# Two rests of the first gate/up chunk on GpSimd, and two rests of later chunks behind the last seven-product pair

## The chip, the cores and the metric

The kernel runs on one core of a Trainium2 chip. The metric is the device time of one execution, in microseconds (us); lower is better. A core has several engines with a queue of instructions each: TensorE (PE) multiplies, VectorE (DVE), ScalarE (ACT) and GpSimd (POOL) work on elements, and SyncE (SP) issues most DMA transfers. Operands lie in SBUF, sums of matmuls in the banks of PSUM.

## The reference

Two layers over 256 tokens of width 2048, in float32. Each layer mixes the tokens (two kinds of attention, one output projection), and then runs a SwiGLU feed-forward part of width 5632. The case is in the second of these lines and what leads up to it:

```python
x = x + rms_norm(mixed, post_mix_norm[l])
h = rms_norm(x, pre_ffn_norm[l])
f = (jax.nn.silu(h @ w_gate[l]) * (h @ w_up[l])) @ w_down[l]
x = x + rms_norm(f, post_ffn_norm[l])
```

## The kernel before

**Numbers in two parts.** TensorE multiplies rounded numbers (the type fp32r). To reach float32 accuracy, every operand is split: `hi` is the value rounded by ACT (L307), `lo` is the rest, raw minus hi, taken as a rule by DVE (L317). I call the first the rounding and the second the rest of a weight. A product a times b becomes three matmuls: hi by hi, hi by lo, lo by hi (`product`, L1131 to L1136, and `eight`, L1252). The activations x have hi and lo as well: `columns` turns a block of x on TensorE (`turned_x`, the PE transposes of L502), ACT rounds the columns with the norm's gain (`rounded_x`, L508), and DVE takes their rests (`rest_of_x`, L516), which read one operand in PSUM and one in SBUF.

**Weights.** All weights stand in DRAM in the order of their use, in pieces of 128 x 1024 (two 128-row blocks by 512 columns, 512 KB), numbered through the whole program. `fetch` loads them by SP's queue into four `raw` buffers (L241), `feed` rounds them and takes their rests into six `hi` and six `lo` buffers. Gate/up has 11 chunks of 512 columns, and in each 8 pairs kp of row blocks, each with a gate weight and an up weight. In layer 0, chunk 0 starts at weight 128, chunk 1 at 144, chunk 2 at 160; the gate weight of a pair has the even number.

**Seven products in place of eight.** Some pairs are computed with a scheme of Strassen's kind: seven block products rather than eight, for sums that DVE must form first. `mixed_weights` (L263) does it for the weights: with gate G and up U, the tile T is U with the first half of G added to its own first half. SP loads U (L257), and an accumulating DMA on GpSimd's queue adds the half of G on top (L258, `accum_op`; it is the row `POOL L258 DMA_DIRECT2D`). Then DVE makes further sums (L290, L291), ACT rounds them (`Th`, L279) and DVE takes their rests (`Tl`, L281): `Tl` of the half T2 first (128 x 512), then of the pair in G (128 x 1024). For x, `pair_sums` adds hi and lo (`f`, L1377, two operands in SBUF) and `token_sums` makes four sums with their rounding (`sh`, L1151) and rests (`sl`, L1152). `seven_products` issues the 21 matmuls; the product p7 (t3) is the first to read the second `Tl`. After the last seven-product pair of a chunk, `shared_part` (L1175 to L1179) puts the four shared sums together for the evacuation of the chunk's banks (L1430 to L1436).

Chunk 0 takes its pairs in the order 0, 1, 3, 2, 7, 4, 6, 5, of which only 6 is a seven-product pair (weights 140 and 141). Chunk 1 takes 0 to 7, with 4, 5, 6 as seven-product pairs; its last is kp 6 (weights 156 and 157), and kp 7 (158 and 159) follows it as an ordinary pair. Chunk 2 has 2, 4, 5, 6 (its last: 172 and 173); chunks 3 to 9 have 2 to 6.

**The order of the work.** A scheduler orders each engine's queue. The code bends it where it names an instruction to issue behind: `tc.issue_after(...)`. The list `held` (an instruction and a count) tells `feed` that the next so many ordinary rests on DVE go behind that instruction; so far it is set once per chunk at the end of `shared_part`. The dictionary `newest_rest` holds each seven-product weight's newest rest, which after `mixed_weights` is the second `Tl`.

**GpSimd.** From chunk 1 on, two rests per chunk run on GpSimd (L310, the list `helped`): the gate weights of the second and third pair of the chunk (in layer 0: 146 and 148, then 162 and 164). The first of them gets a dependency on the newest seven-product matmul, `tc.add_manual_dep(..., reason="the shared port")`. Otherwise GpSimd issues the accumulating DMAs.

**The start of the feed-forward part.** Before chunk 0 a stretch is written out by hand (up to L1325): x is rescaled piece by piece (`rescaled`, L654), turned and rounded, while PE already works on the first pairs. `rounded_next` (L322) rounds the next weight and returns a function that takes its rest on an engine of choice, DVE if none is named. Behind it come the pair kp 3, then the other half of x's columns, the groups cg 3 and 2 for both token blocks t (16 column roundings, 16 column rests), and then the pair kp 2 and the loop over the chunks.

Of the kernel before, what the change touches and what calls it, by code (L numbers as in the profile page):

```python
# [13 lines left out]
ALU = mybir.AluOpType  # L14
# [7 lines left out]
NT = S // P  # L22
# [30 lines left out]
AFTER = mybir.DependencyInfo(mybir.DependencyClass.Sync, mybir.DependencyReason.DATA)  # L53
# [20 lines left out]
def gate_order(c):  # L74

    if c in MORE_AT:
        return MORE_ORDER
    return FIRST_ORDER if c == 0 else tuple(range(KT // 2))


def weight_order():

    order = []

    def queue_pair(name, l, kp, c):
        order.append((name, l, kp, c))
        return len(order) - 1

    plan = []
    sevens, plain, own = set(), set(), set()  # L90
    for l in range(L):
        lay = {"in": {}, "o": {}, "gate": {}, "up": {}, "down": {}}
        for n, (ca, cb) in enumerate(PAIRS):
            for kp in IN_ORDER if n else range(KT // 2):
                lay["in"][ca, kp] = queue_pair("w_in", l, kp, ca)
                lay["in"][cb, kp] = queue_pair("w_in", l, kp, cb)
                if kp in IN_NOW[n]:
                    plain.add(lay["in"][cb, kp])
        order_o = [(c, kp) for kp in KP_O for c in (0, 1)]
        order_o += [(c, kp) for kp in LATE_O for c in (2, 3)] + [(c, kp) for c in (2, 3) for kp in LAST_O]  # L100
        lay["order_o"] = order_o
        for c, kp in order_o:
            lay["o"][c, kp] = queue_pair("w_o", l, kp, c)
            if c == 3 and kp in O_SEVEN:
                own.add(lay["o"][c, kp])
        for c in range(FF // CW):
            for kp in gate_order(c):
                lay["gate"][c, kp] = queue_pair("w_gate", l, kp, c)
                lay["up"][c, kp] = queue_pair("w_up", l, kp, c)
                if kp in gate_sevens(c):  # L110
                    sevens.add(lay["up"][c, kp])
        for half in range(2):
            for kp in range(FF // P // 2):
                for c in (2 * half, 2 * half + 1):
                    lay["down"][c, kp] = queue_pair("w_down", l, kp, c)
                if kp in DOWN_SEVEN[half]:
                    sevens.add(lay["down"][2 * half + 1, kp])
        plan.append(lay)
    return order, plan, sevens, plain, own
# [48 lines left out]
def kernel(  # L168
# [15 lines left out]
    nc = tc.nc  # L184
# [19 lines left out]
    order, plan, sevens, plain, own = weight_order()  # L204
# [3 lines left out]
    for lay in plan:  # L208
        for c in range(1, FF // CW):
            for n in (1, 2):  # L210
                helped[lay["gate"][c, gate_order(c)[n]]] = n == 1
    newest_seven = [None]

    ready = {}
    raws, loads = [], []
# [2 lines left out]
    def fetch(upto):  # L218
        while len(raws) < min(upto, len(stream)):
            i = len(raws)  # L220
            for j in range(i, min(i + EARLY + 1, mix_raw[3])):
                if j in sevens and j not in sums:
                    summed(j)
            if i in sevens:
                raws.append(sums[i])
                continue
            if i + 1 in sevens:
                g = mix_raw[0].tile([P, 2, CW], F32, tag="G", bufs=mix_raw[1], name=f"G{i}")
                with not_ahead(i):
                    loads.append(nc.sync.dma_start(g, stream[i]))  # L230
                raws.append(g)
                continue
            if i in own or i + 1 in own:
                raw = mix_pool[0].tile([P, 2, CW], F32, tag="v", bufs=2, name=f"V{i}")
            elif i in plain or i + 1 in plain:
                raw = late_room([P, 2, CW], f"GU{i}")
            else:
                raw = wpool.tile([P, 2, CW], F32, tag="raw", bufs=4, name=f"raw{i}")
            mixing = bool({i, i + 1} & (own | plain))
            with not_ahead(i) if mixing else nullcontext():  # L240
                loads.append(nc.sync.dma_start(raw, stream[i]))  # L241
            raws.append(raw)
            if not mixing:
                usual.append((i, loads[-1]))
# [18 lines left out]
    def mixed_weights(i):  # L263

        g, u = raws[i - 1], raws[i]
        hi = wpool.tile([P, 2, CW], F32R, tag="hi", bufs=6, name=f"hi{i}")
        lo = wpool.tile([P, 2, CW], F32R, tag="lo", bufs=6, name=f"lo{i}")
        if i in own:
            th = wpool.tile([P, 2, CW], F32R, tag="hi", bufs=6, name=f"Th{i}")
            tl = wpool.tile([P, 2, CW], F32R, tag="lo", bufs=6, name=f"Tl{i}")  # L270
            th2 = mix_pool[0].tile([P, 2 * (S + P)], F32R, tag="ah", bufs=1, name=f"T2h{i}")[:, 0:CW]
            tl2 = mix_pool[0].tile([P, 2 * (S + P)], F32R, tag="al", bufs=1, name=f"T2l{i}")[:, 0:CW]
        else:
            th = mix_pool[0].tile([P, 3, CW], F32R, tag="Th", bufs=1 if i in plain else 2, name=f"Th{i}")
            tl = mix_pool[0].tile([P, 3, CW], F32R, tag="Tl", bufs=1 if i in plain else 2, name=f"Tl{i}")
            th2, tl2 = th[:, 2, :], tl[:, 2, :]

        def split(h, l, w):
            nc.scalar.activation(h, w, AF.Copy)  # L279
            with in_row(i):  # L280
                newest_rest[i] = nc.vector.tensor_tensor(out=l, in0=w, in1=h.bitcast(F32), op=ALU.subtract)  # L281

        if i in plain or i in own:
            with after_rests():
                nc.vector.tensor_tensor(out=u[:, 0, :], in0=g[:, 0, :], in1=u[:, 0, :], op=ALU.add)
        split(hi, lo, u)
        t1, b22 = ((hi[:, k, :], lo[:, k, :]) for k in range(2))
        t3, t4 = ((th[:, k, :], tl[:, k, :]) for k in range(2))
        t2 = u[:, 1, :]
        nc.vector.tensor_tensor(out=t2, in0=t2, in1=u[:, 0, :], op=ALU.subtract)  # L290
        nc.vector.tensor_tensor(out=g, in0=g, in1=t2.unsqueeze(1).to_broadcast([P, 2, CW]), op=ALU.add)  # L291
        split(th2, tl2, t2)
        split(th[:, 0:2, :], tl[:, 0:2, :], g)
        t2 = th2, tl2
        return {"b22": b22, "t1": t1, "t2": t2, "t3": t3, "t4": t4}

# [25 lines left out]
    def rounded_next():  # L322

        i = fed[0]
        fetch(i + 1)
        raw = raws[i]
        hi = wpool.tile([P, 2, CW], F32R, tag="hi", bufs=6, name=f"hi{i}")
        nc.scalar.activation(hi, raw, AF.Copy)
        lo = wpool.tile([P, 2, CW], F32R, tag="lo", bufs=6, name=f"lo{i}")
        ready[i] = (hi, lo)  # L330
        fed[0] += 1

        def rest(eng=nc.vector):
            r = eng.tensor_tensor(out=lo, in0=raw, in1=hi.bitcast(F32), op=ALU.subtract)
            if eng is nc.vector:
                rests.append(r)
            return r

        return rest

    rests = []
    held = [None, 0]
    follows, newest_rest = {}, {}

    def in_row(i):

        return tc.issue_after(follows[i].ins) if i in follows else nullcontext()
# [8 lines left out]
    def after_rests():  # L356

        return tc.issue_after(rests[-1].ins)
# [20 lines left out]
    def x_part(t, a, n):  # L379
        h, a = divmod(a, D // 2)  # L380
        return xs[t][h][:, a : a + n]
# [269 lines left out]

    def rescaled(mg, t, c, r):
        sl = x_part(t, c * CW, CW)
        nc.vector.scalar_tensor_tensor(out=sl, in0=mg[t, c // 2][:, c % 2, :], scalar=r, in1=sl, op0=ALU.mult, op1=ALU.add)  # L654

    def rescale(mg, ssm, t, nm, then=None, newest=None):
        halves = newest is not None
# [527 lines left out]
    for l in range(L):  # L1185
# [11 lines left out]
        mg = {}  # L1197
# [15 lines left out]
        for kp in LATE_O[:-1]:  # L1213
            i, j = (plan[l]["o"][c, kp] for c in (2, 3))
# [23 lines left out]
        def columns(pb, t, cg):  # L1238
            rounded_x(pb, t, cg, g0, xT)
            rest_of_x(pb, t, cg, g0, xT)  # L1240
# [18 lines left out]
        with tc.manual_schedule(engines=by_hand):  # L1259
# [19 lines left out]
            gain(3, 0)  # L1279
            r = [next(root)]  # L1280
            rescaled(mg, 0, 0, r[0])
            last_units(1, (2,))
            pb = [turned_x(0, 0)]
# [46 lines left out]
        for cg in (3, 2):  # L1330
            for t in range(NT):
                with tc.issue_after(newest.ins):
                    rescaled(mg, t, cg, r[t])
                columns(turned_x(t, cg), t, cg)
        eight(first_banks, 0, fourth, range(NT), False, False, ahead=2)
        open_sums[0] = False
# [50 lines left out]
        for c in range(FF // CW):  # L1387
# [47 lines left out]
            for t in range(NT):  # L1435
                nc.vector.scalar_tensor_tensor(  # L1436
                    out=results[c][t], in0=banks[2 * t + 1], scalar=rs[t][:, 0:1], in1=w[2 * t], op0=ALU.mult, op1=ALU.mult
# [9 lines left out]
        mg = {}  # L1447
        ssm = [small.tile([P, 4], F32, tag="ssm", name=f"ssm_d{l}_{t}") for t in range(NT)]
        nkp = FF // P // 2
        for half in range(2):  # L1450
# [74 lines left out]
            for t in range(NT):  # L1525
# [4 lines left out]
                for c in cc:  # L1530
                    for kp in range(nkp - tail, nkp):
# [4 lines left out]
                        for kk in range(2):  # L1536
                            sh, sl = jh[:, kk, t * P : (t + 1) * P], jl[:, kk, t * P : (t + 1) * P]
# [64 lines left out]
```

## Time and profile before

| | us |
|---|---|
| median of 3 runs | 2182.56 (2181.92 to 2182.92) |
| profiled execution | 2184.11 |
| span of its profile | 2182.3 |
| mean granted TensorE clock | 0.998 of full speed |

The profile is of one execution, and all times within it count from the start of its span. In a row of a timeline stand the start, the duration, the engine, the line of the kernel, the operation, what it writes and reads (by the tiles' names, without the buffers' numbers), the shape, how many such instructions the row puts together, and in square brackets how long the engine sat idle before it and what ended that. Rows of waits give: who waits, for what, us in all, times, the longest. Consecutive DVE operations overlap a little in such a view: one of 1.22 us is followed by the next 1.14 us later.

### The profile page before, as it was taken

What the parts mean: (1) busy time and instruction counts of PE and PEld (TensorE: products, weight loads), DVE (VectorE), ACT (ScalarE), POOL (GpSimd) and SP (SyncE); (2) the same over time, 40 slices, a digit from 0 to 9 for tenths busy, and PEclk for the clock granted to TensorE, in tenths of its full rate; (3) what the DMA queues carried; (4) which work ended last, traced back from release to release, by engine and by line L of the source; (5) the groups of instructions that cost most, each with busy time, mean ns of one, the idle gap of its engine ahead of it and who ended that gap; (6) DMA issues with size and microseconds to landing.
All of it is one profiled execution on the core that took longest, in us unless ns stands there. A gap on an engine that the chain in (4) does not pass through costs nothing.

```text
span 2182.3 us, 28785 instructions
## 1 busy us (share of the span) xinstructions
PE 2166.9 (99%) x9950; PEld 1785.7 (82%) x9950; DVE 1922.8 (88%) x2649; ACT 1398.3 (64%) x2085; POOL 254.5 (12%) x241
## 2 busy tenths in 40 slices
PE   9999999999999999999999999999999999999998
PEld 7888888878888888888878888888788888888886
DVE  6888657899999999999878886588999999999997
ACT  7666665756666666666665656657566666576664
POOL 1100000021222220000010000001212212200000
PEclk9999999999999999999999999999999999999999
DMA  9544555588887777767465555546878877768683
GB/s 331 186 165 174 193 184 173 177 280 238 240 261 229 230 230 241 230 228 253 146 241 174 181 172 187 193 154 202 270 232 243 265 226 222 241 227 242 206 267 100
DMA packets 140562, 470.95 MB, mean 216 GB/s; under 512 B 15984, under 2 KB 17008, under 8 KB 139904
## 3 DMA queue, kind: packets, MB, share of 16 engines
q1 hardware_dynamic: 121952, 436.03, 58.1%
q0 software_dynamic: 17888, 32.55, 9.0%
q8 instruction: 78, 1.28, 0.2%
q10 hardware_dynamic: 576, 0.54, 0.1%
q14 instruction: 68, 0.56, 0.1%
HBM read 460.67 MB, written 8.39 MB: 215 GB/s over the span
## 4 chain that ended last, share of the span: by engine, by line
PE 91%; DVE 4%; issue 2%; ACT 1%; DMA 1%; DVEq 0%; SPq 0%; ACTq 0%
PE c L1252 17%; PE in L1134 7%; PE in L1136 7%; PE in L1135 7%; PE dn L1484 4%; PE dn L1486 4%; PE dn L1483 4%; PE p L1135 3%; PE p L1136 3%; PE c L1136 3%; PE c L1135 3%; PE c L1134 3%; PE p L1134 3%; PE o L608 2%; PE o L606 2%; PE o L607 2%
## 5 line engine op out<-in xcount | busy, mean ns | idle before, releaser
L317 DVE TENSOR_TENSOR lo<-raw,hi 128x1024 fp32r<-128x1024 f32 x460 | 552.0, 1221 | 98.7 <-ACT hi L307 94.9
L307 ACT ACTIVATE hi<-raw 128x1024 fp32r<-128x1024 f32 x482 | 492.3, 1053 | 81.2 <-DMA raw<-in_weights_in_turn_dram 34.1
L1252 PE MATMUL c<-hi,xF 128*128 128x512 f32 x1312 | 356.4, 393 | 0.8 <-DVE xF L516 0.5
L1252 PEld LDWEIGHTS c<-hi,xF 128*128 128x128 f32 x1312 | 244.6, 188 | 51.6 <-DVE xF L516 1.3
L258 POOL DMA_DIRECT2D T<-in_weights_in_turn_dram x124 | 109.5, 883 | 1398.8 <-DMA T<-in_weights_in_turn_dram 333.4
L1252 PE MATMUL c<-lo,xF 128*128 128x512 f32 x656 | 202.6, 390 | 0.0
L279 ACT ACTIVATE Th<-G 128x1024 fp32r<-128x1024 f32 x124 | 130.9, 1056 | 76.1 <-DVE G L291 75.1
L1483 PE MATMUL dn<-hi,jh 128*128 128x512 f32 x416 | 162.0, 389 | 0.0
L1484 PE MATMUL dn<-lo,jh 128*128 128x512 f32 x416 | 161.8, 389 | 0.0
L281 DVE TENSOR_TENSOR Tl<-G,Th 128x1024 fp32r<-128x1024 f32 x124 | 151.5, 1222 | 10.0 <-ACT Th L279 10.0
L307 ACT ACTIVATE hi<-G 128x1024 fp32r<-128x1024 f32 x124 | 130.8, 1055 | 45.5 <-DMA G<-in_weights_in_turn_dram 24.8
L281 DVE TENSOR_TENSOR lo<-T,hi 128x1024 fp32r<-128x1024 f32 x124 | 158.1, 1275 | 0.3 <-ACT hi L279 0.2
L291 DVE TENSOR_TENSOR G<-G,T 128x1024 f32<-128x1024 f32 x124 | 151.1, 1218 | 1.8
L279 ACT ACTIVATE Th<-T 128x512 fp32r<-128x512 f32 x124 | 78.5, 633 | 114.0 <-DVE T L290 111.3
L1252 PEld LDWEIGHTS c<-lo,xF 128*128 128x128 f32 x656 | 123.3, 188 | 25.8
L317 DVE TENSOR_TENSOR lo<-G,hi 128x1024 fp32r<-128x1024 f32 x106 | 129.2, 1219 | 9.8 <-ACT hi L307 9.8
L279 ACT ACTIVATE hi<-T 128x1024 fp32r<-128x1024 f32 x124 | 130.2, 1050 | 11.5 <-PE c L1136 9.3
L1134 PE MATMUL in<-hi,xT 128*128 128x512 f32 x328 | 131.8, 404 | 0.8 <-ACT hi L939 0.8
L1134 PE MATMUL in<-hi,xI 128*128 128x512 f32 x328 | 131.1, 401 | 0.0
L1136 PE MATMUL in<-hi,xT 128*128 128x512 f32 x328 | 128.3, 392 | 0.0
L1135 PE MATMUL in<-lo,xI 128*128 128x512 f32 x328 | 128.0, 390 | 0.3 <-DVE lo L317 0.3
L1486 PE MATMUL dn<-hi,jl 128*128 128x512 f32 x416 | 128.0, 389 | 0.0
(487 smaller groups left out, 4954.0 us busy)
## 6 DMA issues: line engine op xcount, KB each, us to landing
raw<-in_weights_in_turn_dram SPq DMA_DIRECT2D x494, 512.0 KB, 4.7
T<-in_weights_in_turn_dram SPq DMA_DIRECT2D x124, 512.0 KB, 5.5
G<-in_weights_in_turn_dram SPq DMA_DIRECT2D x124, 512.0 KB, 5.5
T<-in_weights_in_turn_dram POOLq DMA_DIRECT2D x124, 256.0 KB, 6.2
GU<-in_weights_in_turn_dram SPq DMA_DIRECT2D x32, 512.0 KB, 6.2
V<-in_weights_in_turn_dram SPq DMA_DIRECT2D x8, 512.0 KB, 3.8
away_ffn<-x SPq DMA_DIRECT2D x8, 512.0 KB, 8.2
xd<-away_ffn SPq DMA_DIRECT2D x8, 512.0 KB, 9.0
```

The lines of the kernel that those rows point to most:

```text
L279: nc.scalar.activation(h, w, AF.Copy)
L281: newest_rest[i] = nc.vector.tensor_tensor(out=l, in0=w, in1=h.bitcast(F32), op=ALU.subtract)
L291: nc.vector.tensor_tensor(out=g, in0=g, in1=t2.unsqueeze(1).to_broadcast([P, 2, CW]), op=ALU.add)
L307: nc.scalar.activation(hi, raw, AF.Copy)
L317: rest = nc.vector.tensor_tensor(out=lo, in0=raw, in1=hi.bitcast(F32), op=ALU.subtract)
L1134: nc.tensor.matmul(a, sh, hi, start=first, stop=False, skip_group_check=open_sums[0])
L1135: nc.tensor.matmul(a, sh, lo, start=False, stop=False, skip_group_check=open_sums[0])
L1136: return nc.tensor.matmul(a, sl, hi, start=False, stop=last, skip_group_check=open_sums[0])
L1252: nc.tensor.matmul(a, stat[part], w[j][:, kk, :], start=first and kk + n == 0, stop=last and kk == 1 and n == 2)
L1483: nc.tensor.matmul(accs[c, t], sh, hi[:, kk, :], start=first, stop=False, skip_group_check=open_sums[0])
L1484: nc.tensor.matmul(accs[c, t], sh, lo[:, kk, :], start=False, stop=False, skip_group_check=open_sums[0])
L1486: nc.tensor.matmul(accs[c, t], sl, hi[:, kk, :], start=False, stop=last, skip_group_check=open_sums[0])
```

## The change

It has two parts. In the start of the feed-forward part, all four rescalings of x's second half are issued first. Then the next two weights (kp 4 of chunk 0: 138 and 139 in layer 0, their twins 530 and 531 in layer 1) are rounded on ACT and their rests taken on GpSimd, with a dependency that lets them start only once the last of the rescalings has ended. Then the columns are turned, rounded and their rests taken as before. In `mixed_weights`, behind the last seven-product pair (kp 6) of chunks 1 and 2, `held` is set so that the next two ordinary rests on DVE, those of kp 7, are issued behind that pair's second `Tl`.

```diff
+    last_of_row = {lay["up"][c, 6] for lay in plan for c in (1, 2)}
...
         split(th[:, 0:2, :], tl[:, 0:2, :], g)
+        if i in last_of_row:
+            held[:] = newest_rest[i], 2
...
     def rescaled(mg, t, c, r):
         sl = x_part(t, c * CW, CW)
-        nc.vector.scalar_tensor_tensor(...)
+        return nc.vector.scalar_tensor_tensor(...)
...
         for cg in (3, 2):
             for t in range(NT):
                 with tc.issue_after(newest.ins):
-                    rescaled(mg, t, cg, r[t])
+                    whole = rescaled(mg, t, cg, r[t])
+        for n in range(2):
+            rest = rounded_next()(nc.gpsimd)
+            tc.add_manual_dep(rest.ins, whole.ins.name, AFTER, reason="the shared port")
+        for cg in (3, 2):
+            for t in range(NT):
                 columns(turned_x(t, cg), t, cg)
```

The order in which the two programs issue their work differs as follows. PE's order is the same, instruction by instruction. On DVE, two L317 rests per layer are gone from behind the columns. On GpSimd, two rests per layer are new and stand ahead of the accumulating DMA of weight 141 (533 in layer 1). On ACT, the rounding of 139 stands behind the second of the 16 column roundings instead of behind the last, and the rounding of 141 directly behind that of 140, ahead of four squares of x. At the end of chunk 1, DVE's order was rest 157, rest 158, sum T, rest 159, sum G, first `Tl` of 157, rest 160, second `Tl`, rest 161; it is now rest 157, T, G, first `Tl`, second `Tl`, and then the rests 158 to 161. Chunk 2's end changes in the same way. The loads of weights 162 and 163 wait, before and after, for the buffers that the rests of 158 and 159 read.

More of the change, by code (lines that the diff above doesn't have):

```diff
@@ L653, in rescaled @@
         sl = x_part(t, c * CW, CW)
-        nc.vector.scalar_tensor_tensor(out=sl, in0=mg[t, c // 2][:, c % 2, :], scalar=r, in1=sl, op0=ALU.mult, op1=ALU.add)
+        return nc.vector.scalar_tensor_tensor(out=sl, in0=mg[t, c // 2][:, c % 2, :], scalar=r, in1=sl, op0=ALU.mult, op1=ALU.add)
     def rescale(mg, ssm, t, nm, then=None, newest=None):
```

## The prediction

> **What bounds the kernel now.** I read the page first: the busy shares, then the chain that ended last.
>
> ```profile
> PE 2166.9 (99%) x9950; PEld 1785.7 (82%) x9950; DVE 1922.8 (88%) x2649; ACT 1398.3 (64%) x2085; POOL 254.5 (12%) x241
> ...
> PE 91%; DVE 4%; issue 2%; ACT 1%; DMA 1%; DVEq 0%; SPq 0%; ACTq 0%
> ```
>
> TensorE (PE) is busy 99% of the span, so an edit on VectorE (DVE) and GpSimd (POOL) can gain only where PE waits for them. Next came PE's waits in the gate/up part and PE's timeline at each (columns: start, duration, engine, line, what; in brackets the idle time before it and what ended it).
>
> ```profile
> PE p L1135 <- DVE Tl L281: 3.3, 4, 1.3
> ```
>
> ```profile
> 475.09 0.39 PE L1134 MATMUL p<-Th,sh 128*128 128x512 f32 x1
> 475.95 0.50 PE L1135 MATMUL p<-Tl,sh 128*128 128x512 f32 x1 [0.48 <-DVE Tl L281]
> ...
> 478.23 0.50 PE L1135 MATMUL p<-Tl,sh 128*128 128x512 f32 x1 [1.28 <-DVE Tl L281]
> ...
> 479.26 0.39 PE L1136 MATMUL c<-Th,xF 128*128 128x512 f32 x1
> ```
>
> ```profile
> 1560.58 0.50 PE L1135 MATMUL p<-Tl,sh 128*128 128x512 f32 x1 [0.30 <-DVE Tl L281]
> ...
> 1562.86 0.50 PE L1135 MATMUL p<-Tl,sh 128*128 128x512 f32 x1 [1.28 <-DVE Tl L281]
> ```
>
> ```profile
> 440.00:480.00 40.00, 38.24 (x168) 30.86 (x167) 39.84 (x51) 23.81 (x27) 6.16 (x7) 1.00 0.80 248
> 1563.00:1566.00 3.00, 3.00 (x8) 2.31 (x9) 2.86 (x5) 0.34 (x1) 0.90 (x1) 0.56 1.00 307
> 521.00:850.00 329.00, 329.00 (x1485) 272.91 (x1484) 319.80 (x351) 214.22 (x246) 71.39 (x52) 1.00 0.77 232
> ```
>
> (Windows: busy us of PE, weight loads, DVE, ACT, POOL, then granted clock, DMA share, GB/s.) All four waits stand at one place, twice per layer: the last seven-product pair of gate/up chunk 1 (weight 157, and its twin in layer 1). The last window's 1485 matmuls in 329 us give a pitch of 0.222 us. In layer 0, from 475.09 to 479.26, PE takes 8 steps in 4.17 us, where 8 x 0.222 = 1.78 would do: 2.4 us lost, 1.76 of it idle and 0.6 refill. In layer 1 it is 0.30 + 1.28 idle, the same 0.6, and behind it 3 us at a clock of 0.56, so 3 x 0.44 = 1.3 more: 3.5 us. **The most there is to win is 5.9 us.** DVE causes it: from 440 to 480 it is busy 39.84 of 40 us, so whatever it does earlier shifts the pair.
>
> **Is DVE a bound elsewhere?** From 521 to 850 (chunks 3 to 9) PE never idles, but DVE is at 97%, and its longest waits are its own loop through ACT (us, times, longest):
>
> ```profile
> DVE Tl L281 <- ACT Th L279: 3.9, 7, 0.7
> ```
>
> The end of that stretch shows how far DVE is ahead of PE: the same kind of matmul in chunk 9, and the rest that it uses.
>
> ```profile
> 802.56 0.39 PE L1135 MATMUL p<-Tl,sh 128*128 128x512 f32 x1
> ```
>
> ```profile
> 800.97 1.23 DVE L281 TENSOR_TENSOR Tl<-G,Th 128x1024 fp32r<-128x1024 f32 x1
> ```
>
> ```profile
> 1847.69 0.41 PE L1135 MATMUL p<-Tl,sh 128*128 128x512 f32 x1
> ```
>
> ```profile
> 1846.33 1.22 DVE L281 TENSOR_TENSOR Tl<-G,Th 128x1024 fp32r<-128x1024 f32 x1
> ```
>
> Layer 0: 802.56 - 802.20 = 0.36 us of slack; layer 1: 1847.69 - 1847.55 = 0.14. So a PE that comes out of chunk 1 earlier by 2.4 us meets a DVE that is not earlier by as much, and waits there instead. What is kept is, per layer, the smaller of the stall removed and (slack + G), G being how much earlier DVE itself enters chunk 3.
>
> **The change, part 1: two rests of chunk 0 (weights 138, 139) go to GpSimd.** Per layer DVE loses two of these, starting 1.14 us apart when back to back:
>
> ```profile
> 476.95 1.22 DVE L281 TENSOR_TENSOR Tl<-G,Th 128x1024 fp32r<-128x1024 f32 x1
> 478.09 1.22 DVE L317 TENSOR_TENSOR lo<-raw,hi 128x1024 fp32r<-128x1024 f32 x1
> ```
>
> so 2.3 us off DVE, 4.6 in all. Where they run instead, and GpSimd's price for the same operation:
>
> ```profile
> 414.74 4.22 DVE L516 SCALAR_TENSOR_TENSOR xF<-xT_ps,gains,xF 128x128 fp32r<-128x128 f32 x16
> 418.88 0.75 DVE L1377 TENSOR_TENSOR f<-xF 128x256 f32<-128x256 f32 x2
> ```
>
> ```profile
> 413.56 4.23 ACT L508 ACTIVATE xF<-xT_ps,gains 128x128 fp32r<-128x128 f32 x16 [0.37 <-PE xT_ps L502]
> ```
>
> ```profile
> L310 POOL TENSOR_TENSOR lo<-raw,hi x22: 2382/2450/3813, 436.2 to 1896.1; 128x1024 fp32r<-128x1024 f32 x22
> ```
>
> The first rest may start when the four rescalings end (414.8) and ends by about 417.3, the second by 419.8. PE reads them first here, so they have 6 us of cover:
>
> ```profile
> 426.29 0.62 PE L1252 MATMUL c<-lo,xF 128*128 128x512 f32 x2
> ```
>
> ACT's rounding of weight 139 moves ahead of 14 of the 16 column roundings; that delays those by 1.06, and DVE, which starts 1.2 us behind ACT, by 0.3 at most. Against the saving stand two prices. DVE operations with two SBUF inputs wait for a GpSimd rest: two that take 0.75 alone (row at 418.88) took 3.24 beside one, while the same engine's operations with one PSUM input kept their 0.70 each:
>
> ```profile
> 442.42 3.24 DVE L1377 TENSOR_TENSOR f<-xF 128x256 f32<-128x256 f32 x2
> ...
> 487.01 1.40 DVE L1436 SCALAR_TENSOR_TENSOR act<-c,rs_ffn,w 128x512 f32<-128x512 f32 x2
> ```
>
> ```profile
> 442.34 2.70 POOL L310 TENSOR_TENSOR lo<-raw,hi 128x1024 fp32r<-128x1024 f32 x1
> ...
> 487.54 2.70 POOL L310 TENSOR_TENSOR lo<-G,hi 128x1024 fp32r<-128x1024 f32 x1
> ```
>
> L516 reads PSUM like L1436, so I let it run on; but the second rest (to 419.8) holds up L1377 (due 418.9) by 0.9. And both rests stand on GpSimd's queue ahead of weight 141's accumulating DMA:
>
> ```profile
> 419.15 0.90 POOL L258 DMA_DIRECT2D T<-in_weights_in_turn_dram  x1 [268.42 <-DVE xF L516]
> ```
>
> ```profile
> 422.94 1.06 ACT L279 ACTIVATE hi<-T 128x1024 fp32r<-128x1024 f32 x1 [1.35 <-DMA T<-in_weights_in_turn_dram]
> ```
>
> It goes out at 419.8 in place of 419.15, so ACT's rounding, which waits for that DMA, moves 0.7 back. DVE then idles for it: part of the 2.3 us is lost. I keep 0.8 of it in layer 0 (bounds 0, if the waits eat all, and 2.3). In layer 1 the accumulation followed its columns less closely:
>
> ```profile
> 1498.98 4.23 DVE L516 SCALAR_TENSOR_TENSOR xF<-xT_ps,gains,xF 128x128 fp32r<-128x128 f32 x16
> ```
>
> ```profile
> 1503.96 0.88 POOL L258 DMA_DIRECT2D T<-in_weights_in_turn_dram  x1 [268.98 <-PE c L1252]
> ```
>
> two rests from 1499.0 end at 1504.0, so it is hardly later, and I keep 1.25 (same bounds).
>
> By the Trainium skill (SBUF — State Buffer, "SBUF: two separate sides") the port that DVE and GpSimd share is an exclusive lock, taken for a whole instruction by whichever starts first, and DVE asks for it with two SBUF inputs. That is the rule under which this change would lose what it blocks; by it L1377 pays and L516 does not, as taken above, and no run here shows a rest beside L516.
>
> **Part 2: two rests behind the last pair's.** In chunk 1, three L317 rests now stand behind the pair's Tl: 3 x 1.14 = 3.4 us earlier, less some 0.5 that DVE then waits for ACT's Th (3.9 / 7 in the row above). Tl was ready at 478.17 and needed at 478.23 - 1.28 - 0.48 - 0.5 = 476.0: 2.2 us late, 2.9 us won. The stall goes, even with part 1 at nothing. What is late next: the two rests of kp 7, now ready at some 476.4 and 477.6. PE's work behind the pair, at 479.5 (a step after 479.26) less 2.4, reads them from its fifth matmul on, 477.1 + 4 x 0.222 = 478.0: covered by 0.4, and by more with part 1's lead. They free the buffers that the loads of weights 162 and 163 wait for:
>
> ```profile
> 472.45 0.33 SPq L241 DMA_DIRECT2D raw<-in_weights_in_turn_dram  x1
> ```
>
> ```profile
> 480.20 1.06 ACT L307 ACTIVATE hi<-raw 128x1024 fp32r<-128x1024 f32 x1 [2.38 <-DMA raw<-in_weights_in_turn_dram]
> ```
>
> These go out about 3 us later; ACT's rounding of 163, already waiting for its load, slips to between 481 and 483, and its rest on DVE, at the earliest 480.20 + 1.06 + 1.22 = 482.5 before, comes by 0 to 3 us later; I take 0.7, a quarter, because DVE's shared part of the chunk stands ahead of that rest in any case. But then DVE waited for PE anyway, and PE is now earlier:
>
> ```profile
> 485.81 0.69 DVE L1430 TENSOR_TENSOR w<-c,w 128x512 f32<-128x512 f32 x1 [0.95 <-PE c L1252]
> ```
>
> ```profile
> 1569.77 0.69 DVE L1430 TENSOR_TENSOR w<-c,w 128x512 f32<-128x512 f32 x1 [1.21 <-PE c L1252]
> ...
> 1583.61 1.22 DVE L317 TENSOR_TENSOR lo<-G,hi 128x1024 fp32r<-128x1024 f32 x1 [0.85 <-ACT hi L307]
> ```
>
> So **G**, layer 0: 0.8 - 0.5 - 0.7 + 0.95 + 0.4 = 0.95 (bounds -0.8, if the late load takes all, and 2.0); the 0.4 is an estimate of what is saved because GpSimd's later rests start earlier and block less behind PE's waits (one blocked 3.24 - 0.75 = 2.5; I count a sixth of it). Layer 1: 1.25 - 0.5 - 0.7 + 1.21 + 0.85 + 0.6 = 2.7 (bounds 0.8, 3.6), with a quarter of it.
>
> **The sum.** Layer 0 keeps min(2.4, 0.36 + 0.95) = 1.3; layer 1 min(3.5, 0.14 + 2.7) = 2.8; 4.1 us. Against the profiled execution's 2184.11 (span 2182.3 and 1.8 around it) that is 2180.0; the median of the runs, 2182.56, is 1.55 lower, so **2178.4**. With both layers' lower bounds it is -0.4 + 0.9 = 0.5 us, with the upper ones 5.9.
>
> The drop to 0.56 followed 1.6 us of idle. The Trainium skill (TensorE: Matmul & The Clock Gate, Part 1) ties half rate to a whole idle window of about 3.4 us; by it the drop has another cause and its 1.3 us stay, which makes layer 1's potential 2.2 and the time 2179.1. The trace has the idle beside the drop and cannot say more.
>
> **Rivals.**
> - *DVE is no bound later: all 5.9 are kept, 2176.7.* For it: DVE waits 3.9 us for ACT's Th in chunks 3 to 9, which could shrink. Against: these waits are loops that DVE's own results start, and the slack is 0.36 and 0.14.
> - *The late load of 163 takes DVE's lead: G is -0.2 and 0.9.* Then 0.2 + 1.0 = 1.2 us is kept, 2181.4. For it: ACT already waited 2.38 for that load. Against: DVE's own waits for PE at the same place cover it.
> - *Slower: GpSimd gets no port beside L516.* Its rests would start at 419.0. For it, a rest that had to wait for DVE:
>
> ```profile
> 436.21 3.81 POOL L310 TENSOR_TENSOR lo<-raw,hi 128x1024 fp32r<-128x1024 f32 x1 [16.16 <-ACT hi L307]
> ```
>
> At 2.5 to 3.8 each the accumulation goes out at 424.0 to 426.6, 4.9 to 7.4 late. The last Tl of that pair and its matmul:
>
> ```profile
> 431.59 1.22 DVE L281 TENSOR_TENSOR Tl<-G,Th 128x1024 fp32r<-128x1024 f32 x1
> ```
>
> ```profile
> 434.45 0.39 PE L1135 MATMUL p<-Tl,sh 128*128 128x512 f32 x1
> ```
>
>   have 1.64 between them, and 1.1 come from rounding 141 ahead of other work, so it decides from an accumulation 2.7 late: PE stalls 2.2 to 4.7 there in each layer (in layer 1 with a clock drop of 1.3), DVE enters chunk 1 late by as much, and of the old stall 0.6 stays in each. That is 2 x 2.8 + 1.3 - 5.9 = +1.0 to 2 x 5.3 + 1.3 - 5.9 = +6.0: 2183.6 to 2188.6, about 2186. Against: the 1.40 of L1436.
>
> **How the numbers follow.** Forecast (3.0 to 5.5 us gained, 2177.1 to 2179.6) 0.45; all kept 0.18; lead eaten (0 to 3 us) 0.22; slower 0.12; anything else 0.03. The range reaches from the middle of "all kept" to the lower part of "slower": 2175.8 to 2184.0. A difference of 0.2% is 4.4 us, about what a measurement tells from none. Faster by more: half of the forecast, nearly all of "all kept" and a little else, 0.41. Slower by more: 0.08, the upper half of the slower case and some of the rest. Same: 0.51.
>
> **What would show it.** Right: no PE wait on Tl at weight 157 in both layers and no clock drop behind; two POOL rests of about 2.5 us beside 16 column rests that still take 4.2; 141's accumulation under 1 us later; new, small PE waits on Tl in chunks 3 to 9, some 1 us a layer. Wrong: rests above 3 us beside L516, an idle PE at 434, ACT waiting over 3 us for weight 163, or chunks 3 to 9 with no PE wait though chunk 1's stall is gone.

## The result and the profile after

| | before | changed |
|---|---|---|
| median of 6 runs, us | 2182.74 (2181.92 to 2184.16) | 2192.01 (2188.49 to 2195.45) |
| profiled execution, us | 2184.11 | 2190.8 |
| its span, us | 2182.3 | 2188.8 |

The ratio is 1.0042 with a 95% interval of 1.0029 to 1.0055: 9 us slower (6 to 12), where 4 us faster was forecast. The changed kernel's runs also lie further apart, over 7 us.

Line numbers of the changed kernel are higher by 1 to 8 than those of before (L281 is L282, L317 is L320, L1252 is L1255). First PE's timeline at weight 157 in the profile of the changed kernel.

```profile
475.63 0.39 PE L1137 MATMUL p<-Th,sh 128*128 128x512 f32 x1
475.86 0.39 PE L1138 MATMUL p<-Tl,sh 128*128 128x512 f32 x1
...
476.54 0.39 PE L1138 MATMUL p<-Tl,sh 128*128 128x512 f32 x1
```

The matmuls that read `Tl` follow at full pace: the stall of 0.48 + 1.28 us is gone, in layer 1 too, and the clock there stays at 1.00. The waits of PE in the same profile (us, times, longest) show what came instead.

```profile
PE c L1255 <- ACT act L1378: 5.2, 4, 1.4
...
PE c L1255 <- DVE w L1182: 1.6, 2, 0.8
PE q L1137 <- DVE act L1444: 1.5, 2, 0.8
...
PE c L1255 <- DVE w L1180: 1.0, 2, 0.5
PE p L1138 <- DVE Tl L282: 0.9, 1, 0.9
```

That is 10.2 us of idle time, against the 3.3 us for `Tl` before. By place there are three groups, each in both layers.

**The end of chunk 0** (w L1180 and L1182; in layer 1 also the `Tl` of 533). GpSimd, VectorE and ACT in the profile of the changed kernel:

```profile
413.54 4.77 POOL L337 TENSOR_TENSOR lo<-raw,hi 128x1024 fp32r<-128x1024 f32 x2 [264.30 <-PE xT_ps L505]
418.26 0.88 POOL L259 DMA_DIRECT2D T<-in_weights_in_turn_dram  x1
```

```profile
414.27 4.23 DVE L519 SCALAR_TENSOR_TENSOR xF<-xT_ps,gains,xF 128x128 fp32r<-128x128 f32 x16 [0.95 <-ACT xF L511]
418.42 0.75 DVE L1385 TENSOR_TENSOR f<-xF 128x256 f32<-128x256 f32 x2
...
425.63 1.22 DVE L282 TENSOR_TENSOR lo<-T,hi 128x1024 fp32r<-128x1024 f32 x1 [3.95 <-ACT hi L280]
```

```profile
424.53 1.06 ACT L280 ACTIVATE hi<-T 128x1024 fp32r<-128x1024 f32 x1 [4.31 <-DMA T<-in_weights_in_turn_dram]
```

GpSimd's rests take 2.4 us each beside the 16 column rests, which take 4.23 as before, and the accumulating DMA goes out right behind them, at 418.26. But the rounding of 141 that waits for it starts only at 424.53, and VectorE idles 3.95 us. The DMA issues around it (engine, count, size, median us from issue to landing), before and changed:

```profile
T<-in_weights_in_turn_dram POOLq DMA_DIRECT2D x1, 256.0 KB, 3.6
```

```profile
raw<-in_weights_in_turn_dram SPq DMA_DIRECT2D x2, 512.0 KB, 5.1
T<-in_weights_in_turn_dram POOLq DMA_DIRECT2D x1, 256.0 KB, 6.1
```

SP's queue, before and changed, has those two loads (weights 144 and 145):

```profile
421.23 1.63 SPq L241 DMA_DIRECT2D raw<-in_weights_in_turn_dram  x2
```

```profile
415.98 2.69 SPq L242 DMA_DIRECT2D raw<-in_weights_in_turn_dram  x2
```

The second of the changed kernel's two, by itself:

```profile
418.34 0.33 SPq L242 DMA_DIRECT2D raw<-in_weights_in_turn_dram  x1
```

They refill the buffers of 138 and 139. GpSimd frees these earlier than VectorE did. So one load of 512 KB now goes out 2.3 us ahead of the accumulating DMA and the other together with it (0.08 us behind the start of its issue), where the first followed it by 2.1 us before, and that DMA lands 6.1 us after its issue in place of 3.6 (7.2 in layer 1, 3.7 before).

**The start of chunk 2** (act L1378). ACT and PE in the profile of the changed kernel:

```profile
480.96 1.06 ACT L310 ACTIVATE hi<-raw 128x1024 fp32r<-128x1024 f32 x1 [5.28 <-DMA raw<-in_weights_in_turn_dram]
483.94 1.06 ACT L310 ACTIVATE hi<-raw 128x1024 fp32r<-128x1024 f32 x1 [1.92 <-PE c L1255]
484.90 1.05 ACT L1378 COPY act<-actT_ps 128x512 f32<-128x512 f32 x2
```

```profile
485.52 0.96 PE L1255 MATMUL c<-hi,xF 128*128 128x512 f32 x3 [1.13 <-ACT act L1378]
```

The rounding of 163 (483.94) now follows its late load, and the two copies that empty a PSUM bank stand behind it in ACT's queue. PE waits for that bank.

**The start of chunk 3** (act L1378 again, and act L1444). VectorE's rests behind the last pair, chunk 1 and then chunk 2, and GpSimd, all of the changed kernel:

```profile
475.43 4.63 DVE L320 TENSOR_TENSOR lo<-raw,hi 128x1024 fp32r<-128x1024 f32 x4
...
517.92 6.82 DVE L320 TENSOR_TENSOR lo<-raw,hi 128x1024 fp32r<-128x1024 f32 x4
524.66 0.68 DVE L1179 TENSOR_TENSOR w<-p,w 128x512 f32<-128x512 f32 x1
```

```profile
521.18 2.48 POOL L313 TENSOR_TENSOR lo<-G,hi 128x1024 fp32r<-128x1024 f32 x1 [6.65 <-issue]
```

Four such rests take 6.8 us in chunk 2 and 4.6 in chunk 1. Beside those of chunk 2 GpSimd takes its rest of 178. Before, that rest stood beside the shared part, whose operations read PSUM:

```profile
518.99 2.35 DVE L317 TENSOR_TENSOR lo<-raw,hi 128x1024 fp32r<-128x1024 f32 x2
521.26 0.68 DVE L1176 TENSOR_TENSOR w<-p,w 128x512 f32<-128x512 f32 x1
```

```profile
521.59 2.40 POOL L310 TENSOR_TENSOR lo<-G,hi 128x1024 fp32r<-128x1024 f32 x1 [7.90 <-issue]
```

It missed the last of the four by 0.25 us (521.59 against 521.34). In the change the four would have ended at 522.5 and GpSimd starts at 521.18, so they meet, and the shared part starts at 524.66 and no longer at 521.26. VectorE's next sum T is as much later, ACT waits for it, and one of the two copies that PE waits for stands behind that (ACT of the changed kernel):

```profile
529.35 0.63 ACT L280 ACTIVATE Th<-T 128x512 fp32r<-128x512 f32 x1 [3.26 <-DVE T L291]
529.89 0.57 ACT L1378 COPY act<-actT_ps 128x512 f32<-128x512 f32 x1
```

### The profile page after: what moved, and what is told of

It reads as the page before. It is cut to its first block, busy times and chain, and to the rows that moved or that the text cites. A ratio compares the mean times of both kernels' runs of the same rounds, so it can differ in the third digit from the quotient of the medians.

```text
span 2188.8 us, 28782 instructions
## 1 busy us (share of the span) xinstructions
PE 2167.3 (99%) x9950; PEld 1783.2 (81%) x9950; DVE 1920.9 (88%) x2645; ACT 1396.9 (64%) x2085; POOL 265.5 (12%) x245
## 3 DMA queue, kind: packets, MB, share of 16 engines
q8 instruction: 78, 1.28, 0.2%
## 4 chain that ended last, share of the span: by engine, by line
PE 91%; DVE 4%; ACT 2%; issue 2%; DMA 1%; POOL 0%; DVEq 0%; SPq 0%; ACTq 0%; POOLq 0%
PE c L1255 17%; PE in L1137 7%; PE in L1139 7%; PE in L1138 7%; PE dn L1491 4%; PE dn L1494 4%; PE dn L1492 4%; PE c L1137 3%; PE c L1138 3%; PE c L1139 3%; PE p L1138 3%; PE p L1137 3%; PE p L1139 3%; PE o L609 2%; PE o L611 2%; PE o L610 2%
## 5 line engine op out<-in xcount | busy, mean ns | idle before, releaser
L320 DVE TENSOR_TENSOR lo<-raw,hi 128x1024 fp32r<-128x1024 f32 x456 | 550.9, 1232 | 102.4 <-ACT hi L310 101.4
L1255 PE MATMUL c<-hi,xF 128*128 128x512 f32 x1312 | 357.4, 393 | 8.3 <-ACT act L1378 5.2
L1255 PEld LDWEIGHTS c<-hi,xF 128*128 128x128 f32 x1312 | 243.6, 188 | 61.4 <-ACT act L1378 7.0
L1255 PE MATMUL c<-lo,xF 128*128 128x512 f32 x656 | 202.5, 390 | 0.0
L282 DVE TENSOR_TENSOR lo<-T,hi 128x1024 fp32r<-128x1024 f32 x124 | 157.2, 1268 | 9.3 <-ACT hi L280 9.3
L282 DVE TENSOR_TENSOR Tl<-G,Th 128x1024 fp32r<-128x1024 f32 x124 | 151.8, 1224 | 10.9 <-ACT Th L280 10.9
L1255 PEld LDWEIGHTS c<-lo,xF 128*128 128x128 f32 x656 | 123.0, 188 | 25.8
L320 DVE TENSOR_TENSOR lo<-G,hi 128x1024 fp32r<-128x1024 f32 x106 | 129.7, 1223 | 8.9 <-ACT hi L310 8.5
L1137 PE MATMUL in<-hi,xT 128*128 128x512 f32 x328 | 131.3, 402 | 0.3 <-ACT hi L942 0.3
L1137 PE MATMUL in<-hi,xI 128*128 128x512 f32 x328 | 131.2, 401 | 0.0
L1139 PE MATMUL in<-hi,xI 128*128 128x512 f32 x328 | 128.0, 391 | 0.0
```

Of the source, the lines that this page charges most:

```text
L320: rest = nc.vector.tensor_tensor(out=lo, in0=raw, in1=hi.bitcast(F32), op=ALU.subtract)
L1137: nc.tensor.matmul(a, sh, hi, start=first, stop=False, skip_group_check=open_sums[0])
L1139: return nc.tensor.matmul(a, sl, hi, start=False, stop=last, skip_group_check=open_sums[0])
L1255: nc.tensor.matmul(a, stat[part], w[j][:, kk, :], start=first and kk + n == 0, stop=last and kk == 1 and n == 2)
```

## The experiments

All differences in time are (ratio - 1) times the median of before on the same chips, with the 95% interval.

| kernel | median, us | difference, us |
|---|---|---|
| the change | 2192.01 | +9.2 (+6.3 to +12.0) |
| e1: both orders, nothing on GpSimd | 2188.67 | +4.1 (+2.2 to +6.1) |
| e2: GpSimd part alone | 2185.34 | +2.0 (0 to +3.9) |
| e3: chunk 1's order alone | 2184.69 | +1.1 (-0.9 to +3.1) |
| e4: GpSimd part and chunk 1's order | 2186.29 | +3.1 (+1.1 to +5.0) |
| g1: e2, two loads held | 2179.82 | -3.3 (-5.2 to -1.3) |
| g3: e4, two loads held | 2181.77 | -2.0 (-3.9 to 0) |
| h1: the change, two loads held | 2187.36 | +3.5 (+1.5 to +5.2) |
| g2: e1, GpSimd's rest of 178 later | 2210.8 | +25.8 (+22.7 to +28.8) |
| h3: g3, copies ahead of the rounding of 163 | 2182.78 | 0 (-2.0 to +2.0) |
| h2: g1, sums for kp 4 earlier | 2177.99 | -5.5 (-7.4 to -3.3) |
| i1: those sums earlier, alone | 2180.65 | -2.0 (-3.9 to 0) |
| i2: h2, sums for kp 5 earlier too | 2180.23 | -2.8 (-4.8 to -0.9) |

A second table gives VectorE's lateness against the profile of before, from the ends of the same instructions in each timeline: A is the stretch from the rest of 137 to that of 157, B from there to the end of chunk 2's shared part (529, 549 in layer 1). Before, A is 471.29 - 412.16 = 59.13 us and B 524.06 - 471.29 = 52.77 in layer 0. In A, e1 and e3 have before's order and differ from it by -0.3 to +1.0: so far one execution can be trusted. The column "rule" is the difference in time that the prediction's rule makes of A and B. Per layer, PE keeps the smaller of the stall (2.4, 3.5) and the slack (0.36, 0.14) plus VectorE's lead, and the lead is A + B with the sign turned; what is kept counts as minus.

| us, layer 0 / layer 1 | A | B | rule | measured |
|---|---|---|---|---|
| the change | +1.4 / +2.2 | +3.5 / +2.1 | +8.7 | +9.2 |
| e1 | +0.3 / -0.3 | +3.2 / +1.8 | +4.4 | +4.1 |
| e2 | +1.4 / +0.8 | +0.1 / -1.6 | +0.1 | +2.0 |
| e3 | +1.0 / +0.4 | +0.4 / +0.5 | +1.7 | +1.1 |
| e4 | +1.4 / +0.8 | +0.5 / -2.0 | +0.2 | +3.1 |
| g1 | -0.9 / -1.3 | 0.0 / -0.8 | -3.5 | -3.3 |
| g3 | -0.9 / -1.3 | +0.3 / -0.1 | -2.5 | -2.0 |
| h1 | -0.9 / -1.3 | +3.0 / +2.0 | +2.3 | +3.5 |
| g2 | +0.5 / +0.7 | +0.9 / -1.0 | +0.7 | +25.8 |
| h3 | -0.7 / -1.3 | +1.1 / -0.5 | -1.9 | 0 |
| h2 | -1.6 / -2.4 | +0.4 / -1.3 | -5.1 | -5.5 |
| i1 | -1.0 / -0.5 | +0.2 / -1.3 | -3.0 | -2.0 |
| i2 | -0.3 / -1.4 | +0.1 / -1.5 | -3.6 | -2.8 |

Nine of the thirteen agree with the measured difference within 1.2 us, and all but g2 within 3. In those nine, how late VectorE ends chunk 2 accounts for the difference in time.

### The parts one by one: e1, e2, e3, e4

e1 is before with the lines on `last_of_row` alone; e3 the same for chunk 1 only; e2 is the change without them; e4 the change with chunk 1 only:

```diff
-    last_of_row = {lay["up"][c, 6] for lay in plan for c in (1, 2)}
+    last_of_row = {lay["up"][c, 6] for lay in plan for c in (1,)}
```

> The two rests of chunk 0 stay on VectorE; only the order behind the last seven-product pair of chunks 1 and 2 is changed. Theory A (two separate costs): in the profile of the changed kernel the stall at weight 157 is gone in both layers (about -5.4 us together), but PE waits anew at the start of chunk 2 (1.1 and 1.5 us) and twice at the start of chunk 3 (2.1 and 2.1 us), because the loads behind kp 7's rests go out late. Then this kernel has those waits and not the ones at the end of chunk 0: about +1 to +3 us against before, 2184 to 2186. Rival B (the GpSimd part makes VectorE late and everything behind follows from it): the new waits of chunks 2 and 3 are gone here, and the time is about 2178.

> Only the two rests of chunk 0 go to GpSimd; the order at the end of chunks 1 and 2 is that of before. Theory A: PE waits 1.3 us at the end of chunk 0 in both layers (VectorE's shared part late, because the accumulating DMA of weight 141 lands 6.1 us after its issue in place of 3.6, with two weight loads sent out ahead of it), and the old stall at weight 157 stays: +3 to +5 us, about 2187. Rival B: the whole loss is here, 2190 or more. Rival C (the GpSimd part does what the prediction said, a lead for VectorE): the stall at 157 shrinks, 2180 to 2182.

> Only the order at the end of chunk 1 is changed. Theory A: the stall at 157 is gone (-5.4), PE waits 1.1 to 1.5 per layer at the start of chunk 2 for ACT's copies behind the late rounding of weight 163, and chunk 3's start is as before: about -3 us, 2179 to 2181. If the late loads of chunk 1 alone cost as much as they bring, 2182 to 2184.

> The change without its reordering of chunk 2. Theory A: after's time less the two waits at the start of chunk 3 in each layer (2.6 to 3.2 us a layer): 2184 to 2187. Rival B: no better than the changed kernel, about 2191.

The waits stay where their part stays, with one exception. PE in e1 waits at the starts of chunks 2 and 3, as in the change; e2 has the waits at the end of chunk 0. The exception is e4: with chunk 1's order, it has no wait for copies at chunk 2. The first copy is as late there (484.79 against 484.90 in the change), but PE itself comes about 1 us later, by its waits at the end of chunk 0. Sizes differ from theory A's by 1 to 3 us (e1 lost more than it expected, e2 less). So rival B, one lateness behind all, falls. Rival C's sign came in part: the stall at 157 is 0.58 and 0.57 us in e2, in place of 1.76 and 1.58. But PE loses more than that ahead of it, 2.0 and 1.8 us at the end of chunk 0 (waits for the `Tl` of 141 and 533 included), and VectorE is later (A), so C falls as well. The order of chunk 1 alone, expected at -3, comes to +1.1: it removes the stall and gives it all back. In layer 1 of e3 its ACT and PE show where PE waits instead:

```profile
1570.04 1.06 ACT L310 ACTIVATE hi<-raw 128x1024 fp32r<-128x1024 f32 x1 [3.51 <-DMA raw<-in_weights_in_turn_dram]
1571.00 1.05 ACT L1373 COPY act<-actT_ps 128x512 f32<-128x512 f32 x2
```

```profile
1571.62 1.50 PE L1255 MATMUL c<-hi,xF 128*128 128x512 f32 x3 [2.63 <-ACT act L1373]
```

The load of 555 (163's twin) is late here too, and PE idles 2.63 us for the copies behind its rounding. Chunk 2's order costs 4.1 - 1.1 = 3.0 us of time and, in B, 2.8 and 1.3 us of VectorE: the larger of the two, and no stall stood there to be won.

### The two loads held: g1, g3, h1

The loads of 144 and 145 wait for VectorE's rest of 140, which brings them back to about where they were (421.57 against 421.23); no engine's order changes.

```diff
+    after_lo = {lay[w][1, 0]: lay["gate"][0, 6] for lay in plan for w in ("gate", "up")}
...
+            if i in after_lo:
+                tc.add_manual_dep(loads[-1].ins, placed[after_lo[i]].ins.name, AFTER, reason="behind the sum's load")
```

Here `placed` keeps each ordinary rest by its weight.

> The kernel with only the GpSimd part, and the load of weight 144 (and with it 145 behind it in SP's queue; 536 and 537 in layer 1) waits for VectorE's rest of 140, as late as it went out before. Theory A (the accumulating DMA of 141 lands 6.1 us after its issue in place of 3.6 because the loads that GpSimd's early rests release go out ahead of it): it lands within 4 us again, PE's waits at the end of chunk 0 (0.5 and 0.8 us per layer) are gone or under 0.3, and the time falls by 2 to 3 us against the GpSimd part alone, to about that of before or 1 us below. Rival (the order on ScalarE, four squares between the rounding of 141 and that of the sums, makes VectorE late): the waits stay.

> The same held loads, with the order of chunk 1 changed as well. Theory A: against before, the stall at 157 gone and no waits at the end of chunk 0: 1 to 3 us below before, 2180 to 2182, less what ScalarE's copies behind the rounding of 163 cost. Rival: no better than without the held loads, 2186.

> The changed kernel in full, with the loads of weights 144 and 145 (536, 537) as late as they were before. Theory A: its two costs are separate, so only the GpSimd part's is taken away (5 us between the GpSimd part alone and the same with held loads): about before's time, 2183 to 2186, with no PE waits at the end of chunk 0 and still 1 to 1.5 us waits at the start of chunks 2 and 3. Rival B (one lateness of VectorE behind all waits): the waits at chunks 2 and 3 go as well, 2180 or less.

GpSimd, SP and ACT of g1, and its DMA:

```profile
418.30 0.87 POOL L262 DMA_DIRECT2D T<-in_weights_in_turn_dram  x1
```

```profile
421.57 8.21 SPq L243 DMA_DIRECT2D raw<-in_weights_in_turn_dram  x3
```

```profile
422.12 1.06 ACT L283 ACTIVATE hi<-T 128x1024 fp32r<-128x1024 f32 x1 [1.87 <-DMA T<-in_weights_in_turn_dram]
```

```profile
T<-in_weights_in_turn_dram POOLq DMA_DIRECT2D x1, 256.0 KB, 3.7
```

The accumulating DMA goes out at the same time as in the change (418.30 against 418.26) and lands 3.7 us later instead of 6.1; the rounding starts at 422.12, 2.4 us earlier, with the same four squares behind it, so the rival that blamed ScalarE's order falls. PE's waits at the end of chunk 0 are gone. Three pairs of kernels differ by this edit alone, and it is worth 2.0 + 3.3 = 5.3, 3.1 + 2.0 = 5.1 and 9.2 - 3.5 = 5.7 us, where 2 to 3 were expected of the first. GpSimd's part by itself is then a gain of 3.3 us, where 1 us at most was expected; VectorE's lead in A is 0.9 and 1.3 us. h1 stays above what theory A gave it (2187.36 against 2186 at most), and its waits at chunks 2 and 3 stay too, so rival B falls here as well. What stays in it is the two orders: 3.5 + 3.3 = 6.8 us above g1, of which chunk 1's is 3.3 - 2.0 = 1.3 and chunk 2's 3.5 + 2.0 = 5.5.

### What the orders cost by: g2 and h3

g2 is e1 with one more dependency: the GpSimd rest that stood beside chunk 2's four rests starts after the shared part. (`held_off` holds weights 178 and 570, `shared_end` the last instruction of the shared part.)

```diff
+                if i in held_off:
+                    tc.add_manual_dep(rest.ins, shared_end[0].ins.name, AFTER, reason="the shared port")
```

> Both reorderings without the GpSimd part (VectorE is 2.6 us late at chunk 2's end there), and the GpSimd rest of weight 178 (570 in layer 1) may start only after the shared part of chunk 2. If that rest, by holding up one of the four rests that now stand ahead of the shared part, is what costs: the four take 4.6 us in place of 6.8 and PE's waits at the start of chunk 3 (1.4 and 0.8 us per layer) shrink below 0.5; about 3 us less than with both reorderings alone, 2185 to 2186. If it is the order alone (two more rests ahead of the shared part): the waits stay, 2188 or more.

VectorE in g2:

```profile
516.66 4.62 DVE L324 TENSOR_TENSOR lo<-raw,hi 128x1024 fp32r<-128x1024 f32 x4
...
525.17 2.77 DVE L293 TENSOR_TENSOR T<-T 128x512 f32<-128x512 f32 x1
```

The four rests take 4.6 us again, so the 2.2 us were GpSimd's; but the rest then holds up the sum T, 2.77 us in place of 0.69. PE's waits at the start of chunk 3 do not shrink (1.51, 1.04 and 1.00 us in layer 0). Later orders changed too (ACT's differs from e1's in over 100 places), to 26 us slower, so g2 is no clean test of the time. The mechanism is shown, the saving is not: in both places where that rest stood beside VectorE's operations with two SBUF inputs, it cost them 2.1 to 2.2 us.

h3 is g3 with ACT's rounding of 163 behind the two copies (weight 163 is fed one step later, and issued behind `copied`, the last copy):

```diff
+            with tc.issue_after(copied[0].ins) if i in behind_copies else nullcontext():
+                nc.scalar.activation(hi, raw, AF.Copy)
```

> The GpSimd part with held loads and the order of chunk 1 changed, and ScalarE's rounding of 163 (555) behind the two copies of the turned activations instead of ahead of them. If the copies wait only because the late rounding stands ahead of them: PE's wait for them (1.5 us at the start of chunk 2 in layer 1) is gone, 2179 to 2181, about 1 us less than without. If PE then waits for VectorE in chunks 3 to 9 (slack of the last rests there already 0.05): no gain in time, 2181 to 2182, the wait only moves.

PE's waits in h3:

```profile
PE p L1146 <- DVE Tl L288: 2.9, 3, 1.3
```

The wait for the copies is gone, so they did wait for nothing but the late rounding. In its place PE waits 2.9 us for `Tl`, and no time is won: 2182.78 against 2181.77, or 0 against -2.0 us from before.

### Where VectorE's lead comes from: h2, i1, i2

```diff
-FORM_AT = {(0, 2): (6,), (0, 4): (4,), (0, 5): (5,), (1, 3): (2,), (2, 4): (3,)}
+FORM_AT = {(0, 2): (6, 4), (0, 5): (5,), (1, 3): (2,), (2, 4): (3,)}
```

h2 is g1 with this line, i1 is before with it, and i2 is h2 with (0, 4): (5,) as well.

> The GpSimd part with held loads, and the sums of x for kp 4 formed where VectorE idles for weight 141 (1.5 us of work in a gap of about 2). If VectorE's lead at chunk 3 sets what is kept (the step of the prediction that the kept gain is slack plus lead): 1 to 2 us less than with held loads alone, 2178 to 2179, and the stall at 157 under 0.5 us. If PE's own stall at 157 sets it: no change beyond 0.5 us.

> The kernel before with the sums of x for kp 4 formed one step earlier, and nothing on GpSimd: VectorE's idle time ahead of weight 141 (1.9 us per layer before) takes 1.5 us of its work. If the gain of the GpSimd part with held loads and earlier sums (-5.5 us) is the sum of two leads of VectorE: half of it or less here, 2180.5 to 2182.5. If the earlier sums alone do it: 2178.

> As the version with held loads and earlier sums, and the sums for kp 5 formed earlier too, so that they no longer stand beside GpSimd's rest of weight 148, which makes two operations take 3.2 us in place of 0.75. If those 2.5 us are lost lead: 1 to 2 us less, 2176.5 to 2177.5. If that rest then holds up the next operation with two SBUF inputs instead: no change within 1 us.

h2 is the fastest of all: 5.5 us below before, with PE's waits for `Tl` down to this row:

```profile
PE p L1140 <- DVE Tl L285: 0.5, 1, 0.5
```

The sums alone bring 2.0 us, held GpSimd rests alone 3.3, together 5.5: two leads of VectorE that add up. i2, expected within 1 us of h2 or below it, comes out 2.7 us above (the intervals overlap). VectorE in i2 shows why the sums for kp 5 gain nothing:

```profile
442.95 3.08 DVE L321 TENSOR_TENSOR lo<-raw,hi 128x1024 fp32r<-128x1024 f32 x1
```

GpSimd's rest of 148 now holds up the next rest instead, 3.08 in place of 1.22. And PE has a new wait for chunk 0's shared part, one in each layer, which h2 does not have:

```profile
PE c L1257 <- DVE w L1184: 1.6, 2, 0.8
```

## Why the prediction was wrong

**The bound: right.** The stall at weight 157 and the clock drop behind it were there to be won, VectorE's lateness caused them, and the reordering removed both. (The drop is seen in the one profile of before, where it went on beyond the 3 us that were counted: the clock was 0.87 from 1566 to 1569. g1, which keeps 1.2 us of the stall in each layer, shows none.)

**The accumulating DMA: the step that failed first.** "It goes out at 419.8 in place of 419.15, so ACT's rounding, which waits for that DMA, moves 0.7 back": the issue was right (418.26, in a timeline that ran some 1.5 us ahead), the rounding was not. The step counted the queue that the DMA stands in and not the loads that the early rests release into SP's queue, one ahead of it and one with it. It was 2.4 us that they cost VectorE in layer 0, by the two starts of the rounding in the change and in g1, and 5 to 6 us of time in both layers together. With them held back, the leads that the step kept, 0.8 and 1.25 us, are there: 0.9 and 1.3. In the prediction's terms it is G that failed: a lead of 0.95 and 2.7 us was forecast, and the change has a lateness (A + B) of 4.9 and 4.3.

**The late load of 163: part 2's gains did not come.** The load goes out 3.7 us later (477.86 against 474.19, in timelines that agree within 0.2 us at the rest of 157), so its rounding starts beyond the 481 to 483 that the prediction allowed (483.94), and its rest ends 3.0 us later. The prediction took 0.7 us for that and set against it what VectorE would no longer wait; with both, part 2 came to a lead of 0.15 and 1.46 us. In e3, B shows a lateness of 0.4 and 0.5. Also, "DVE's own waits for PE at the same place cover it" looked at one queue: the copies behind the rounding on ACT held PE for 1.1 to 2.6 us in e1, e3 and the change. That this wait is what e3's time was lost by is not shown, for h3 takes it away and gains nothing. What the table shows is that chunk 1's order gave VectorE no lead, so the rule lets PE keep none of the stall.

**Chunk 2's order: not priced.** The prediction had the change's second `held` in no term of its sum, as no stall stood at chunk 2. It cost 3.0 us on top of e3, 5.5 on top of g3 and 6.1 on top of e4, so up to as much as the early loads. The same four rests stand ahead of the shared part before and after, but now in a row behind the pair's sums and later, and GpSimd's rest, which had stood beside the shared part, fell beside one of them.

**Slack plus lead: right.** What PE kept was what VectorE was early by, as the column "rule" shows: the rule holds, and its input G was wrong. In g1, chunk 9's last rest is ready 0.05 us ahead of the matmul that reads it (0.36 before). PE and VectorE of g1:

```profile
801.07 0.50 PE L1140 MATMUL p<-Tl,sh 128*128 128x512 f32 x1
```

```profile
799.79 1.23 DVE L285 TENSOR_TENSOR Tl<-G,Th 128x1024 fp32r<-128x1024 f32 x1
```

So PE runs against VectorE there (801.07 - 801.02), and h3, which takes a wait from PE and gives VectorE nothing, gains nothing.

**The rivals.** "Slower" came true by another mechanism, and further out than its 2183.6 to 2188.6: GpSimd had its port beside L516 all along, at 2.4 us a rest. The nearest was the late load, with the right cause and the wrong victim. "All kept" is out: no version kept the whole stall without a lead on VectorE.

**What stays open.** e1's and e2's differences sum to 6.1 us, the change's is 9.2; the intervals overlap. The orders cost more on top of GpSimd's part (9.2 - 2.0 = 7.2 us, and 6.8 with held loads) than alone (4.1); why is not shown. e4 lost 2.9 us more than the rule gives. Why the runs of the changed kernel spread over 7 us was not tried.

## What to carry to other kernels

An operation that finishes earlier also frees its input earlier, and the transfer that waited for the buffer starts earlier: look up what it will then be ahead of or beside. On an in-order queue, price a late input by everything behind its first reader, not by that reader alone. Where a second engine is nearly saturated over a long stretch, a stall removed ahead of the stretch is kept only as far as that engine becomes earlier too, so taking work off it or filling its idle time is worth more than moving its work about.

## What was not expected of the hardware

The same 256 KB accumulating DMA took 3.6 to 3.8 us from issue to landing where the next two loads of 512 KB went out 1.5 us or more behind it (before, e1, e3, g1, g3 and h1, both layers). It took 6.1 to 7.2 where one of them went out 2.3 us ahead and the other with it (the change, e2 and e4).

PE's granted clock did not follow every idle: in e3's layer 1 it fell to 0.56 after one wait of 2.63 us, as it had before the change after 0.30 + 1.28 us, and in the changed kernel it stayed at 1.00 after one of 1.45 us. Windows of e3, and of the changed kernel (PE, weight loads, DVE, ACT, POOL, clock, DMA share, GB/s):

```profile
1571.50:1574.00 2.50, 2.38 (x6) 1.89 (x7) 2.50 (x4) 1.57 (x4) 0.89 (x1) 0.56 1.02 418
```

```profile
1575.50:1578.00 2.50, 2.22 (x10) 1.81 (x11) 2.50 (x4) 1.57 (x4) 0.89 (x1) 1.00 1.03 416
```

By the Trainium skill (TensorE: Matmul & The Clock Gate, Part 1) half rate takes a whole idle window of about 3.4 us. Both drops here follow idle times shorter than that, so the rule as stated does not cover them.
